# Output projection of a hybrid encoder layer: seven products of quarters in place of eight, with the residual added on GpSimd

## The chip, the cores and the metric

The kernel runs on one core of a Trainium2 chip. The core has a matrix engine (TensorE, PE in the profile, with its weight loads as PEld), a vector engine (VectorE, DVE), an activation engine (ScalarE, ACT), GpSimd (POOL) and SyncE (SP), which here only issues DMAs. Each engine works through its own queue in order; semaphores join them. The metric is the device time of one execution in microseconds, and the median of several executions is compared.

## The reference

One layer: a pre-norm, one input projection, two mixers that run side by side (chunked band attention and a gated delta rule), an output projection with a residual, and a feed-forward block with a residual. The part at issue is the output projection:

```python
mixed = jnp.concatenate([o_att, o_dn], axis=-1) @ w_out[layer]
h = h + mixed
z = rms_norm(h, ffn_norm_gain[layer]) @ w_ff1[layer]
h = h + jnp.square(jax.nn.relu(z)) @ w_ff2[layer]
```

Tokens, model width and the width of the two mixers together are all 1024, so the projection is a product of two 1024 x 1024 matrices in float32.

## The kernel before, in words

Everything is kept transposed: features on the 128 partitions, tokens along the rows. A float32 product is made of three matmuls: `split` (L201) writes a rounded copy of an operand with a cast on ACT (the high part) and the rest with a subtract on DVE (the low part), and `mm3` (L217) multiplies high by high, low by high and high by low.

The mixers leave four quarters in SBUF, each 512 features by 512 tokens: `mix[0][0]` and `mix[1][0]` from the attention (names `mixa0`, `mixa1`), `mix[0][1]` and `mix[1][1]` from the delta rule (`mixd0`, `mixd1`); the first index is the half of the tokens. `out_weights` (L1193) loads a half of W_out's columns, eight blocks of 128 x 512, through three buffers (tag `wr`). `out_proj` (L1199) makes four quarters of h, `R[j, hf]` (half j of the features, half hf of the tokens), each of four row tiles of 128 x 512: a row tile takes eight blocks of 128 times three matmuls in one PSUM bank; DVE adds the residual x to it on the way out (L1229), ACT squares it, POOL sums the squares (L1236), a DMA stores the quarter (L1237), and ACT scales it by the gain of the next norm (L1239) for the feed-forward block. The order is (0,0), (1,0), (1,1), (0,1), 384 matmuls in all.

The projection begins while the last units of the attention and of the delta rule still run. `attention` takes the generator's first steps (at most 30) as filling for PE between the units' own steps; the last unit is `t17`, the second group of four heads at token tile 7. Its normalization goes from PE (`t17_o`, then the transposes `t17_on`) through DVE, ACT (a square with its sum) and POOL (an inverse square root in small steps `t17_v`, `t17_y`, `t17_t`, `t17_r`) back to DVE, to PE (the transposes `t7_tpo`), and to DVE (L1070), which writes the last tile of `mixa1`. The order of instructions on each engine is set when the program is built, by a scheduler that simulates it; `issue_after` and priorities in the code shape it. PSUM for the projection is a pool of three banks, taken in turn.

The feed-forward block already uses seven products in place of eight for its matrices (`product` in `ff1` and `ff2`); it begins with `R[0, 0]`, goes on with `R[1, 0]`, and its first DVE work on sums of quarters is at L1290.

Of the kernel before, what the change touches and what calls it, by code (L numbers as in the profile page):

```python
# [14 lines left out]
P = 128  # L15
# [21 lines left out]
SPREAD = 5  # L37
WARM = 11
# [60 lines left out]
def hymba_kernel(  # L99
# [106 lines left out]
    lo_turn = [0]  # L206

    def load_w(src, name, tags=("wh", "wl"), low=None):
        raw = page("wr", name + "_r")
        nc.sync.dma_start(out=raw, in_=src)  # L210
        hi = page(tags[0], name + "_h", F32R)
        lo = page(tags[1], name + "_l", F32R)
        lo_turn[0] += 1
        split(raw, hi, lo, nc.scalar, low or (nc.gpsimd if lo_turn[0] % 2 else nc.vector))
        return hi, lo
# [977 lines left out]
    def out_weights(w, j):  # L1193
        w.append([None] * NKT)
        for k in order:
            w[j][k] = load_w(w_out[k * P:(k + 1) * P, j * 512:(j + 1) * 512], f"wo{j}_{k}",
                             (("wh", "u"), ("u", "wl"))[j], nc.vector)

    def out_proj(result, w):  # L1199


        parts, R, begun = [], {}, []

        def mixed(hf):
            parts.append([None] * NKT)
            low = [quarter(f"ml1{b}", F32R) for b in range(2)] if hf else None
            for j, k in enumerate(order):
                src = part(mix[hf][k // 4], k % 4)
                hi = page("u" if hf else ("pp", "cv")[k // 4], f"mh{hf}{k}", F32R)
                lo = part(low[k // 4], k % 4) if hf else page("dk", f"ml{hf}{k}", F32R)  # L1210
                with ExitStack() as queue:
                    if not hf:
                        for copies in turned:
                            queue.enter_context(tc.issue_after(copies[j // 2 - SPREAD]))
                    split(src, hi, lo, nc.scalar, nc.vector)
                parts[hf][k] = hi, lo

        def rows(j, hf, acc):
            R[j, hf] = r = quarter(f"h{j}{hf}")
            for i in range(4):  # L1220
                n = f"op{j}{hf}{i}"
                s = slice(i * P, (i + 1) * P)
                xt = page("wr", n + "_x")
                nc.sync.dma_start(out=xt, in_=x_t[4 * j + i, :, hf * TH:(hf + 1) * TH])
                ps = bank(ps_a, n)
                for m, k in enumerate(order):
                    mm3(ps, [((w[j][k][0][:, s], w[j][k][1][:, s]), parts[hf][k])], m == 0, m == NKT - 1)
                    yield
                nc.vector.tensor_tensor(part(r, i), ps, xt, ALU.add)  # L1229
                if i == 0 and acc is None:  # L1230
                    acc = page("on", n + "_q")
                    begun.append(nc.scalar.activation(acc, part(r, i), AF.Square).ins)
                else:
                    sq = page("wh", n + "_q")
                    nc.scalar.activation(sq, part(r, i), AF.Square)  # L1235
                    nc.gpsimd.tensor_tensor(acc, acc, sq, ALU.add)  # L1236
            nc.sync.dma_start(out=h_dr[j, hf], in_=q4(r))  # L1237
            for i in range(4):
                nc.scalar.mul(part(r, i), part(r, i), fgain[:, 4 * j + i:4 * j + i + 1])  # L1239
            return acc  # L1240

        mixed(0)
        acc = yield from rows(0, 0, None)
        out_weights(w, 1)
        acc = yield from rows(1, 0, acc)
        nc.sync.dma_start(out=sq_dr[:, 0:TH], in_=acc)
        mixed(1)
        acc = yield from rows(1, 1, None)
        acc = yield from rows(0, 1, acc)
        nc.sync.dma_start(out=sq_dr[:, TH:SEQ], in_=acc)  # L1250
# [425 lines left out]
```

## Time and profile before

| | |
|---|---|
| median of 3 runs | 1267.04 us (1262.9 to 1267.42) |
| the profiled execution | 1262.15 us, of which its span 1260.4 us |
| granted TensorE clock | 0.998 |
| chain that ended last | PE 55%, DVE 5%, ACT 1%; `op L222` (the projection) 7% |
| output projection, first to last matmul | 542.1 to 636.9 us |
| its matmuls | 3 x 128 of 128x512 |

In the profile an L number is a line of the kernel, `out<-in` are the names of the tiles without their numbers, and `xN` counts instructions. The chain of work that ended last is followed back from the last instruction to what released it at each step; where it stays on PE for long, PE had no pause. The output projection's matmuls are the rows `op L222`, its casts and subtracts the rows L203 and L204 with `wo`, `mh` and `ml`.

### The profile page before, as it was taken

To read this page: it belongs to the slowest core of one execution; us is meant where nothing else is said; L and a number is where in the kernel's file an instruction comes from. 1 tells how busy PE (TensorE), PEld (TensorE's weight loads), DVE (VectorE), ACT (ScalarE), POOL (GpSimd) and SP (SyncE) were. 2 spreads that over 40 slices of the span, in tenths; PEclk is the share of its full clock that TensorE was granted. 3 is DMA by queue.
4 is the path that set the end of the run, shared out by engine and by line. 5 is a ranking of instruction groups with operands and counts; after the bars stand their busy time and mean duration, and the time that the engine had idled before them with its cause. 6 is when DMAs were issued, how large, how long until landed. Compare 5 with 4: busy or idle time off the path is not lost.

```text
span 1260.4 us, 17948 instructions
## 1 busy us (share of the span) xinstructions
PE 1237.4 (98%) x6686; PEld 1030.8 (82%) x6686; DVE 929.2 (74%) x1397; ACT 547.4 (43%) x899; POOL 278.3 (22%) x478
## 2 busy tenths in 40 slices
PE   9999999999999999899999999999999999999997
PEld 8778878788789898788888788888887888888886
DVE  7899987754227568776269766767769997997998
ACT  8233132242236666665355444454445543333330
POOL 4425461343223445533200000000000000000043
PEclk9999999999999999999999999999999999999999
DMA  7214353664676532145242343333259624332002
GB/s 228 65 42 137 101 155 93 142 155 117 192 232 167 169 105 76 35 126 170 89 142 99 103 133 118 117 133 102 71 202 377 197 70 134 102 99 101 1 34 100
DMA packets 134375, 158.53 MB, mean 126 GB/s; under 512 B 31120, under 2 KB 78224, under 8 KB 133776
## 3 DMA queue, kind: packets, MB, share of 16 engines
q1 hardware_dynamic: 116192, 135.11, 35.3%
q10 hardware_dynamic: 18096, 22.29, 5.2%
q8 instruction: 52, 0.85, 0.3%
q14 instruction: 35, 0.29, 0.1%
HBM read 109.91 MB, written 47.45 MB: 125 GB/s over the span
## 4 chain that ended last, share of the span: by engine, by line
PE 55%; DVE 5%; ACT 1%; issue 1%; POOL 0%; DVEq 0%
PE p L1444 23%; PE q L1348 20%; PE op L222 7%; PE t_o L1026 1%; DVE h L1290 1%; PE t_sa L927 0%; DVE q_0a_l L204 0%; PE t_tpb L987 0%; PE t_tpa L1003 0%; PE t_sb L927 0%; ACT t_pb L966 0%; PE c_pv L516 0%; PE c_po L516 0%; PE t_tpo L520 0%; PE c_pq L516 0%
## 5 line engine op out<-in xcount | busy, mean ns | idle before, releaser
L1516 POOL TENSOR_TENSOR y<-y,y 128x1024 f32<-128x1024 f32 x4 | 11.5, 2896 | 575.6 <-DVE y L1512 570.8
L1512 DVE TENSOR_TENSOR y<-y,p 128x1024 f32<-128x1024 f32 x46 | 55.1, 1214 | 5.1 <-PE p L1444 4.1
L222 PE MATMUL op<-ml,wo_h 128*128 128x512 f32 x128 | 50.2, 395 | 0.0
L222 PE MATMUL op<-mh,wo_h 128*128 128x512 f32 x128 | 49.2, 393 | 0.8 <-ACT mh L203 0.8
L222 PE MATMUL op<-mh,wo_l 128*128 128x512 f32 x128 | 49.2, 391 | 0.0
L947 DVE CUSTOM_DVE_ANT_0 t_pb<-t_sb,biasn 128x256 f32<-128x256 f32 (+1 forms) x64 | 23.2, 400 | 30.1 <-DMA vt<-v_dr 27.0
L966 ACT ACTIVATE t_pb<-t_pb,t_nm 128x256 f32<-128x256 f32 (+1 forms) x64 | 31.4, 491 | 17.5 <-DVE t_nm L958 16.0
L1236 POOL TENSOR_TENSOR op_q<-op_q 128x512 f32<-128x512 f32 x14 | 20.7, 1478 | 54.6 <-ACT op_q L1235 54.3
L1229 DVE TENSOR_TENSOR h<-op,op_x 128x512 f32<-128x512 f32 x16 | 10.8, 687 | 29.2 <-PE op L222 29.1
L222 PEld LDWEIGHTS op<-mh,wo_h 128*128 128x128 f32 x128 | 23.9, 188 | 6.4 <-ACT mh L203 1.0
L222 PEld LDWEIGHTS op<-ml,wo_h 128*128 128x128 f32 x128 | 24.0, 188 | 5.1 <-DVE ml L204 0.2
L222 PEld LDWEIGHTS op<-mh,wo_l 128*128 128x128 f32 x128 | 24.1, 188 | 5.0
L222 PE MATMUL g_ps<-uh,wg_h 128*128 128x512 f32 x64 | 25.3, 396 | 1.5 <-ACT wg_h L203 1.5
L958 DVE CUSTOM_DVE_ANT_0 t_pa<-t_sa,biaso,t_nm 128x384 f32<-128x384 f32 (+2 forms) x48 | 24.9, 543 | 2.3 <-PE t_sa L927 2.0
L970 ACT ACTIVATE t_pa<-t_pa,t_nm 128x384 f32<-128x384 f32 (+2 forms) x48 | 26.4, 550 | 0.0
L927 PE MATMUL t_sb<-ks,t_q 128*128 128x256 f32 (+1 forms) x144 | 23.9, 294 | 1.9 <-DVE t_nm L947 1.3
L222 PE MATMUL g_ps<-uh,wg_l 128*128 128x512 f32 x64 | 25.2, 393 | 0.4 <-POOL wg_l L204 0.4
L222 PE MATMUL aq_ps<-waq_h,uh 128*128 128x512 f32 x64 | 25.5, 399 | 0.0
L222 PE MATMUL dq_ps<-uh,wdq_h 128*128 128x512 f32 x64 | 25.5, 398 | 0.0
L222 PE MATMUL dv_ps<-uh,wdv_l 128*128 128x512 f32 x64 | 25.4, 397 | 0.0
L222 PE MATMUL aq_ps<-waq_l,uh 128*128 128x512 f32 x64 | 25.3, 395 | 0.0
L222 PE MATMUL dq_ps<-ul,wdq_h 128*128 128x512 f32 x64 | 25.3, 395 | 0.0
(1110 smaller groups left out, 4302.7 us busy)
## 6 DMA issues: line engine op xcount, KB each, us to landing
wa<-in_w_ff_dram SPq DMA_DIRECT2D x32, 512.0 KB, 3.9
a<-in_w_ff_dram SPq DMA_DIRECT2D x32, 512.0 KB, 3.8
b<-f_dr SPq DMA_DIRECT2D x32, 512.0 KB, 3.4
f_dr<-yy ACTq DMA_DIRECT2D x16, 512.0 KB
t_q<-q_dr SPq DMA_DIRECT2D x30, 256.0 KB, 4.1
f_dr<-zz ACTq DMA_DIRECT2D x13, 512.0 KB
ks<-k_dr SPq DMA_DIRECT2D x16, 256.0 KB, 5.3
wo_r<-in_w_out_dram SPq DMA_DIRECT2D x16, 256.0 KB, 5.2
```

The costliest lines, as they stand in the source:

```text
L222: nc.tensor.matmul(ps, a, b, start=(first and i == 0), stop=(last and i == n - 1))
L927: nc.tensor.matmul(o, q[m][:, i * P:(i + 1) * P], k[:, c], start=(m == 0), stop=(m == 1))
L947: nc.vector.tensor_tensor_reduce(sb[:, c], bk[:, c], new[g][pp][:, c], -1.0, 3.0e38, ALU.add, ALU.min, nm[:, 4 + i:5 + i])
L958: nc.vector.tensor_tensor_reduce(sa[e][:, 0:wa], bk[:, 0:wa], old[g][i][:, 384 - wa:384], -1.0, nm[:, 4 + i:5 + i], ALU.add, ALU.min, nm[: ...
L966: nc.scalar.activation(sb[:, c], sb[:, c], AF.Exp, bias=m, scale=-1.0, accum_out=T["sums"][:, 4 + i:5 + i])
L970: nc.scalar.activation(sa[e][:, 0:wa], sa[e][:, 0:wa], AF.Exp, bias=m, scale=-1.0, accum_out=T["sums"][:, i:i + 1])
L1026: return nc.tensor.matmul(po[64 * e:64 * e + 64, pp * P:(pp + 1) * P], vt[k0 + j][:, 64 * h:64 * h + 64], (ta[e] if j < na else tb)[:, c:c ...
L1236: nc.gpsimd.tensor_tensor(acc, acc, sq, ALU.add)
L1290: nc.vector.tensor_tensor(t, wide(R[a], i), wide(R[b], i), ALU.subtract)
L1348: nc.tensor.matmul(part(ps, q), l[:, s], r, start=(k + m == 0), stop=(k == 3 and m == 2))
L1444: nc.tensor.matmul(part(ps[q], 0) if by_rows else part(ps[q // 2], q % 2), l[:, s], part(r, k), start=(i + k + m == 0), stop=(i + k + m == 4))
L1512: nc.vector.tensor_tensor(y[i][m], y[i][m], ps[m], op)
```

## The change

The product of the two matrices, each cut into quarters, is computed by Winograd's form of Strassen's scheme: seven products of quarters (p1, p2, p5, p6, p7, p4, p3 in the order of the program) with sums and differences of quarters in front of and behind them. A product has four row tiles of four blocks times three matmuls, 48 in all. W_out's quarters a11, a12, a21, a22 are loaded anew for the sums (`s1` = a21 + a22, `s2` = s1 - a11, `s3` = a11 - a21, `s4` = a12 - s2); those of the mixers are combined in place (`t1` to `t4`). s1 and s2 are made on POOL, the other differences on DVE; all eight blocks of operands of a product are split on ACT and DVE. DVE or ACT empty the banks into `oy1` and `oy5` (partial results) and into the quarters of h; POOL adds the residual x to them, block by block, and joins `oy5` and `oy1`. The loads for the sums go through the two-buffer pages that the delta rule (`jq`, `jv`, `jg`) and the attention (`raw`) used. The loads of the feed-forward weights are issued behind the first load of x.

The diff, cut to its core:

```diff
+        def product(n, a, b, use):
             for i in range(4):
                 s = slice(i * P, (i + 1) * P)
+                ps = bank(ps_a, f"{n}_{i}")
+                for m in range(4):
+                    mm3(ps, [((a[m][0][:, s], a[m][1][:, s]), b[m])], m == 0, m == 3)
                     yield
+                use(i, ps)
...
+        def residual(t, j, hf, i, tag="wr"):
+            xt = page(tag, f"x{j}{hf}{i}", w=516 if tag == "raw" else 512)[:, 0:512]
+            ins = nc.sync.dma_start(out=xt, in_=x_t[4 * j + i, :, hf * TH:(hf + 1) * TH]).ins
...
+            nc.gpsimd.tensor_tensor(t, t, xt, ALU.add)
...
+        def done(j, hf, last):
+            nc.sync.dma_start(out=h_dr[j, hf], in_=q4(R[j, hf]))
             for i in range(4):
+                nc.scalar.mul(part(R[j, hf], i), part(R[j, hf], i), fgain[:, 4 * j + i:4 * j + i + 1])
...
+        def use2(i, ps):
...
+            tt(part(R[0, 0], i), part(y1, i), ps, ALU.add)
+            residual(part(R[0, 0], i), 0, 0, i)
+            squared(0, 0, i)
...
+        def use6(i, ps):
+            tt(part(y1, i), part(y1, i), ps, ALU.add)
+            nc.gpsimd.tensor_tensor(y5[i], y5[i], part(y1, i), ALU.add)
+            residual(part(y1, i), 1, 0, i)
+
+        def use7(i, ps):
...
+            tt(part(R[1, 1], i), y5[i], ps, ALU.add)
+            tt(part(y1, i), part(y1, i), ps, ALU.add)
+            residual(part(R[1, 1], i), 1, 1, i, J[i])
+            residual(y5[i], 0, 1, i, J[i])
+            squared(1, 1, i)
...
+        yield from product("p1", w[4:8], lo[0:4], use1)
+        yield from product("p2", w[0:4], lo[4:8], use2)
+        done(0, 0, False)
...
+        for m in range(4):
+            with tc.issue_after(w_loads[-1]):
+                r1, r2 = raw(J[m], "a21", 1, 0, m), raw(J[m], "a22", 1, 1, m)
+            S.append(page("pp" if m < 3 else "cv", f"os{m}"))
+            nc.gpsimd.tensor_tensor(S[m], r1, r2, ALU.add)
+            a.append(halves(S[m], f"s1{m}", "u", "wl"))
+            tt(part(b11, m), part(b12, m), part(b11, m), ALU.subtract)
+            b.append(halves(part(b11, m), f"t1{m}", "u", "u"))
+        yield from product("p5", a, b, use5)
...
+            nc.gpsimd.tensor_tensor(S[m], S[m], r1, ALU.subtract)
+            a.append(halves(S[m], f"s2{m}", "wl", "u"))
+            tt(part(b11, m), part(b22, m), part(b11, m), ALU.subtract)
+            b.append(halves(part(b11, m), f"t2{m}", "pp", "dk"))
+        yield from product("p6", a, b, use6)
...
+        yield from product("p7", a, b, use7)
+        done(1, 1, False)
...
+        yield from product("p4", a, b, use4)
+        done(1, 0, True)
...
+        yield from product("p3", a, b, use3)
+        done(0, 1, True)
```

How the built order moves, at the three places that count. The first is the end of the attention on PE. Before, around the transposes `t17_on`, with `op003` and `op100` row tiles of the projection:

```order
L222 MATMUL op003_6760<-mh03_6622,wo0_3_h_6416 128x512
L222 MATMUL op003_6760<-ml03_6623,wo0_3_h_6416 128x512
L1051 MATMUL t17_on_6652<-ident_138,t17_pb1_6347 128x128 x2
L222 MATMUL op003_6760<-mh03_6622,wo0_3_l_6417 128x512
L222 MATMUL op100_6845<-mh04_6594,wo1_4_h_6796 128x512
L222 MATMUL op100_6845<-ml04_6595,wo1_4_h_6796 128x512
```

and around `t7_tpo`, 42 projection matmuls later:

```order
L222 MATMUL op102_6907<-mh05_6598,wo1_5_h_6802 128x512
L222 MATMUL op102_6907<-ml05_6599,wo1_5_h_6802 128x512
L520 MATMUL t7_tpo_6717<-ident_138,t04_on_4606 128x128 x4
L222 MATMUL op102_6907<-mh05_6598,wo1_5_l_6803 128x512
L222 MATMUL op102_6907<-mh06_6602,wo1_6_h_6808 128x512
```

And now, with `p2_2` and `p2_3` the third and fourth row tile of product p2:

```order
L223 MATMUL p2_2_6762<-ml3_6624,wo0_3_h_6416 128x512
L223 MATMUL p2_2_6762<-mh3_6623,wo0_3_l_6417 128x512
L1052 MATMUL t17_on_6650<-ident_138,t17_pb1_6347 128x128 x2
L521 MATMUL t7_tpo_6715<-ident_138,t04_on_4606 128x128 x4
L223 MATMUL p2_3_6782<-mh0_6611,wo0_0_h_6398 128x512
```

The matmuls between the two transposes are gone; p2_3 takes the bank of p2_0 and waits for DVE's `h00<-oy1,p2_0`. On DVE and POOL the last unit's steps now stand among the operands of the next products. DVE now, from the scale of `t04_on` (the tile that `t7_tpo` transposes) on, with `c11_r` and `c21_r` freshly loaded blocks of W_out:

```order
L1328 TENSOR_TENSOR c11_r1_7063<-c11_r1_7063,c21_r1_7065 128x512
L1061 TENSOR_SCALAR t04_on_4606<-t04_on_4606,t17_r_6661 128x512
L205 TENSOR_TENSOR s30_l_7054<-c11_r0_7048,s30_h_7053 128x512
L1328 TENSOR_TENSOR c11_r2_7078<-c11_r2_7078,c21_r2_7080 128x512
L1328 TENSOR_TENSOR c11_r3_7093<-c11_r3_7093,c21_r3_7095 128x512
L1071 TENSOR_TENSOR mixa1_6201<-t7_tpo_6715,again_286 128x4x128
L1267 TENSOR_TENSOR h00_6735<-oy1_6594,p2_0_6722 128x512
```

POOL now, where before a single 128x512 sum of squares stood between `t17_v` and `t17_r`:

```order
L1309 TENSOR_TENSOR os3_6856<-a21_r3_6852,a22_r3_6854 128x512
L188 TENSOR_SCALAR t17_v_6656<-t17_oss_6654 128x1
L1318 TENSOR_TENSOR os0_6811<-os0_6811,b11_r0_6927 128x512
L1318 TENSOR_TENSOR os1_6826<-os1_6826,b11_r1_6939 128x512
L190 TENSOR_TENSOR t17_y_6658<-t17_v_6656,mhalf_151 128x1
L1318 TENSOR_TENSOR os2_6841<-os2_6841,b11_r2_6951 128x512
L1318 TENSOR_TENSOR os3_6856<-os3_6856,b11_r3_6963 128x512
L193 TENSOR_TENSOR t17_t_6660<-t17_y_6658 128x1
```

Five blocks of POOL work stand in front of or among the small steps. The second place is ACT ahead of product p6, whose operands are the splits of `s2` and `t2`; `sq003` is the square of the last tile of `R[0, 0]`, `t30_h` to `t33_h` and `s32_h` are high parts for p7, `oy5_2` a result of p5:

```order
L1249 ACTIVATE sq003_6799<-h00_6735 128x512
L204 CAST t30_h_7058<-mixd1_5953 128x512
L204 CAST t31_h_7073<-mixd1_5953 128x512
L204 CAST t32_h_7088<-mixd1_5953 128x512
L204 CAST t33_h_7103<-mixd1_5953 128x512
L1273 COPY oy5_2_6910<-p5_2_6897 128x512
L204 CAST s32_h_7083<-c11_r2_7078 128x512
```

DVE splits the same blocks in this order, and its four low parts of `t2` (`t20_l` to `t23_l`) stand behind them; p6's third matmul reads `t20_l`. The third place is ACT ahead of product p3. Before, the scaling of a stored quarter stood among squares of later tiles:

```order
L1235 ACTIVATE op113_q_7120<-h11_6999 128x512
L1239 ACTIVATE h11_6999<-h11_6999,fgain_278 128x512 x4
L1235 ACTIVATE op010_q_7157<-h01_7128 128x512
L1235 ACTIVATE op011_q_7188<-h01_7128 128x512
L1235 ACTIVATE op012_q_7219<-h01_7128 128x512
```

Now the high parts of p3's operands (`s40_h`, `b220_h`) are behind it:

```order
L1249 ACTIVATE sq102_7296<-oy1_6594 128x512
L1255 ACTIVATE h11_7120<-h11_7120,fgain_278 128x512 x4
L204 CAST q2_0a_h_7585<-wa12_0_7508 128x1024
L1249 ACTIVATE sq103_7313<-oy1_6594 128x512
L204 CAST s40_h_7325<-e12_r0_7322 128x512
L204 CAST b220_h_7329<-mixa1_6201 128x512
```

The scaling waits for the store of `h11`, and the store for POOL's residual add to `h11`'s last tile; p3's first matmul reads `b220_h` and `s40_h`.

140 lines of the change are left out of this document (88 added, 52 removed).

## The prediction

> **What bounds the kernel now.** The page's first part comes first, then the stage of the output projection by itself, since the change is worth what that stage makes of it: the busy times of its window and PE's waits in it.
>
> ```profile
> PE 1237.4 (98%) x6686; PEld 1030.8 (82%) x6686; DVE 929.2 (74%) x1397; ACT 547.4 (43%) x899; POOL 278.3 (22%) x478
> ...
> 541.00:637.00 96.00, 95.19 (x463) 77.96 (x462) 46.17 (x67) 42.48 (x74) 27.40 (x33) 1.00 0.39 126
> ...
> PE op L222 <- ACT mh L203: 0.8, 1, 0.8
> ```
>
> PE is busy 95.19 of the 96 us of the stage and waits there once, 0.8 us. DVE has 46.17 us of work in it, ACT 42.48, POOL 27.40: half or less. So a matmul that is left out is worth its full pitch here, as long as the other engines keep delivering. The chain that ended last shows that pitch, and the end of the stage:
>
> ```profile
> 562.53 2.34 PE t_o L1026 x40
> 564.87 5.44 PE op L222 x23
> ...
> 570.53 9.56 PE op L222 x42
> 580.09 0.44 PE t_tpo L520 x4
> 580.53 56.46 PE op L222 x247
> 636.98 5.24 PE q L1348 x23
> ...
> 645.47 0.49 DVE h L1290
> ...
> 570.15 0.38 PE L1051 MATMUL t_on<-ident,t_pb 128*128 128x128 f32 x2
> ```
>
> 56.46 / 247 = 0.229 us for a 512-column matmul. From `t_o`, the last attention product, to the first feed-forward matmul PE runs without a pause. Note the third row: between the transposes `t_on` (570.15, the last row, from the timeline) and `t_tpo` (580.09) of the last attention tile PE had 42 projection matmuls. They cover that tile's normalization.
>
> **What is removed.** Seven products of 48 matmuls stand for eight: 48 x 0.229 = **11.0 us** less for PE. 79 matmuls stand ahead of `t_o` where 72 did, so `t_o` ends (T0 below) about 1.5 us later and 257 matmuls are left behind it.
>
> **What is added.** Loads of W_out rise from 16 to 36, the splits and differences are on ACT and DVE, and POOL gets 28 adds of 128x512 beside its 14 sums of squares. Their prices:
>
> ```profile
> L1236 POOL TENSOR_TENSOR op_q<-op_q x14: 1281/1294/2356, 563.2 to 638.6; 128x512 f32<-128x512 f32 x14
> ...
> L203 ACT CAST wo_h<-wo_r x16: 604/620/622, 522.2 to 581.1; 128x512 fp32r<-128x512 f32 x16
> ...
> 585.96 3.59 DVE L204 TENSOR_TENSOR ml<-mixd,mh 128x512 fp32r<-128x512 f32 x4
> ...
> 586.85 1.55 POOL L1236 TENSOR_TENSOR op_q<-op_q 128x512 f32<-128x512 f32 x1 [8.87 <-ACT op_q L1235]
> ...
> 589.47 2.48 DVE L204 TENSOR_TENSOR ml<-mixa,mh 128x512 fp32r<-128x512 f32 x4
> ```
>
> A POOL add is 1.29 us alone, a DVE subtract 2.48 / 4 = 0.62, a cast 0.62 (0.55 in a row of several). The same four subtracts take 3.59 with one POOL add among them: 1.11 more, nearly the whole add. **POOL and DVE take turns on operands in SBUF.** POOL now has some 40 such operations in about 80 us, DVE some 64 (39.7 us).
>
> Three waits of PE follow from the order of the rows.
>
> **W1, in front of product p2's last row tile.** PE now has `t7_tpo` straight behind `t17_on`: the 42 matmuls that covered it are gone, and p2_3 needs the bank that DVE empties only behind `mixa1`. The durations of that normalization:
>
> ```profile
> 574.47 0.19 POOL L187 TENSOR_SCALAR t_v<-t_oss 128x1 f32<-128x1 f32 x1 [8.63 <-ACT t_on L1058]
> 574.74 0.56 POOL L189 TENSOR_TENSOR t_y<-t_v,mhalf 128x1 f32<-128x1 f32 x1
> ...
> 576.51 0.64 POOL L192 TENSOR_TENSOR t_t<-t_y 128x1 f32<-128x1 f32 x1
> ...
> 577.79 0.19 POOL L199 TENSOR_TENSOR t_r<-t_y,t_t 128x1 f32<-128x1 f32 x1
> ...
> 578.01 0.49 DVE L1060 TENSOR_SCALAR t_on<-t_on,t_r 128x512 f32<-128x512 f32 x1 [0.91 <-POOL t_r L199]
> ...
> 582.47 0.69 DVE L1070 TENSOR_TENSOR mixa<-t_tpo,again 128x512 f32<-128x512 f32 x1
> ...
> 566.49 0.33 SPq L210 DMA_DIRECT2D wo_r<-in_w_out_dram  x1
> ...
> 569.08 0.62 ACT L203 CAST wo_h<-wo_r 128x512 fp32r<-128x512 f32 x1 [1.43 <-DMA wo_r<-in_w_out_dram]
> ...
> wo_r<-in_w_out_dram SPq DMA_DIRECT2D x13, 256.0 KB, 5.2
> ```
>
> Counted from T0: the load `a22_r3` goes into a buffer that `t_o` reads to its end, and lands 2.6 later (569.08 - 566.49) at 2.7. Everything on PE stands behind p2_3, so nothing runs in the meantime. POOL's row then is os3 (to 4.0), `t17_v` (4.2, its square long done), two adds (6.8), `t17_y` (7.4), two adds (10.0), four small steps (1.5, as from 576.51 to 577.98) to 11.5. DVE's follows: scale 0.49, three subtracts 1.9, `mixa1` and the first `h00` 0.69 each: 15.2. Eight splits and differences of DVE fall between POOL's adds, up to 5.0 us if all of them hold POOL up; DVE often waits there for its own inputs, so I take half: 17.7. PE has 5 matmuls, `t_on` and `t_tpo` to do meanwhile, 1.9. **W1 = 15.8**; 13.3 with nothing shared, 20.9 with all of it and a load of 5.2.
>
> **W2, in front of p6.** Counted from the start of p2_3, p5 ends at 60 x 0.229 = 13.7, and two matmuls of p6 run to 14.2. The third needs `t20_l`. DVE has it behind the splits of p7's operands; those wait for ACT's `t30_h`; in front of that ACT has `sq003`, which waits for the fourth residual add. POOL's seven adds (9.0) and DVE's twelve subtracts (7.4) are 16.4 one after the other; then come `sq003` and `t30_h` (1.2), five ACT operations to `s32_h` (2.75), five DVE splits (3.05): 23.4, a wait of 9.2. Were nothing shared, the add would follow DVE's 9.4 at once: 17.7 and a wait of 3.5. I take **W2 = 8**, near the shared end, since both queues are full there as in the row of 3.59.
>
> **W3, in front of p3.** ACT's rows put the scaling of `h11` ahead of `s40_h`, and the scaling waits for `h11`'s store. The rows for it:
>
> ```profile
> h_dr<-h SPq DMA_DIRECT2D x4, 1024.0 KB, 5.5
> ...
> 578.15 2.56 ACT L1239 ACTIVATE h<-h,fgain 128x512 f32<-128x512 f32 x4 [2.70 <-DMA h_dr<-h]
> ...
> 615.04 1.05 ACT L203 CAST q_0a_h<-wa 128x1024 fp32r<-128x1024 f32 x1 [4.08 <-PE op L222]
> ```
>
> Counted from the end of p6: PE is free after 96 x 0.229 = 21.9. POOL starts when DVE has emptied p6_0 (18 matmuls before the end, 0.69 to empty it), at -3.4; `h11`'s last residual is its 16th operation: 20.6 later, 17.2, and up to 6.8 more for eleven DVE operations between them; half is 20.6. Store 5.5, scaling 2.56, one cast of 1024 columns 1.05 and three operations of 0.62: 31.6. **W3 = 9.7** (6.3 to 13.1). Before, PE had enough work at this place.
>
> PE's restart after such a wait is not in this trace; its nearest rows are the launch:
>
> ```profile
> 1.05 5.07 PE L165 MATMUL warm<-ones 128*128 128x128 f32 x22 [1.05 <-POOL ones L160]
> ...
> 5.77 0.77 PE L362 MATMUL dk_ps<-uh,wdk_h 128*128 128x512 f32 x1
> 6.34 0.63 PE L362 MATMUL dk_ps<-ul,wdk_h 128*128 128x512 f32 x1
> 6.77 0.52 PE L362 MATMUL dk_ps<-uh,wdk_h 128*128 128x512 f32 x1
> 7.13 0.40 PE L362 MATMUL dk_ps<-ul,wdk_h 128*128 128x512 f32 x1
> ...
> PE p L1444 <- DVE p50b_l L204: 1.8, 1, 1.8
> ...
> 960.25 293.64 PE p L1444 x1294
> ```
>
> The first 22 matmuls take 0.21 us each where `t_tpo`'s take 0.11, and the next three 0.57, 0.43, 0.36 instead of 0.229: about 3 us lost from a standing start. Behind the 1.8 us wait there is no loss to see (293.64 / 1294 = 0.227). So a restart costs 0 to 3; I take 1.3 each behind W2 and W3 (behind W1 it only eats into W2), 2.5 in all. The Trainium skill, "TensorE: Matmul & The Clock Gate", part 1, says that an idle window of some 3.4 us halves the clock, and that as long a busy one restores it. By that each restart would lose 1.7 (an estimate from that page) and the forecast would be 0.9 higher; no wait of this trace is long enough to show it, though the launch agrees.
>
> The first feed-forward products have their operands in time: `b11` is split before p3 ends, and DVE's full stretch starts 8.5 us behind the stage's end, as before (row 645.47 of the chain against 636.98), give or take 1.
>
> **Sum.** -11.0 + 15.8 + 8 + 9.7 + 2.5 = **+25.0**. With nothing shared and no restart: -11.0 + 13.3 + 3.5 + 6.3 = +12.1. With everything: -11.0 + 20.9 + 9.2 + 13.1 + 6 = +38.2. The profiled execution took 1262.15, which gives 1287. The median of the runs shown, 1267.04, is 4.9 above it; for a median of new runs I add half of that: **1289**.
>
> **Rivals.**
> - A: POOL and DVE hardly disturb each other in these places. The other row for it is 1281, POOL's shortest, at a quiet DVE. +12.1: 1274 to 1280. Chance 0.20.
> - B: not slower. Its mechanism is POOL's queue at W3 and W2: if POOL works off its adds while PE stands in W1, only W1 is left, and at a floor of 11 (operands early, no DVE row in between) it equals the saving: 1262 to 1267. It decides itself at W3 where `h11`'s last add is done by 10.9 after p6 (21.9 - 5.5 - 2.56 - 2.9): 16 adds in 14.3 us, 0.9 each, below the shortest row of 1281. The busy tenths speak for it, the rows against it. Chance 0.12, a third of it faster.
> - C: full turns everywhere, loads of 5.2 and slow restarts: +38.2, 1296 to 1306. Chance 0.16. The Trainium skill, "SBUF — State Buffer", section on the two separate sides, calls the port pair of VectorE and GpSimd an exclusive lock: the loser blocks for a whole instruction. By that rule alone the shared ends of the three waits hold (18.3, 9.2, 13.1), an estimate of +32 with my restarts; the rows of 3.59 and 1.55 bear the rule out, but not that both queues are full throughout.
>
> **How the numbers follow.** My forecast holds 0.52 (1280 to 1296), A 0.20, C 0.16, B 0.12. The range 1274 to 1306 leaves out B and the tails of C. Half a per cent, 6.3 us, is about what a measurement of this kernel can tell from no change. Faster by more has a third of B, 0.04; within it 0.08; slower by more 0.88.
>
> **What would show it.** In the changed profile: PE waits of over 10 us at `t_tpo` and at p2 on DVE or POOL; one of some 8 at p6 on a DVE split of `t2`, one of some 9 at p3 on ACT, with ACT waiting for a store of `h`; POOL's 128x512 adds at 1.5 us or more in the mean; the first `q` matmul some 25 us later. If PE's waits between `t_o` and `q` sum to under 17 us, the forecast is wrong; if they come from loads that land late, the reason is.

## The result, and the profile after

The changed kernel takes **1297.2 us** in the median (1295.88 to 1299.5, four runs) where the kernel before takes 1267.23 beside it: a ratio of **1.0251** (95 % interval 1.0236 to 1.0266). It is slower by 2.5 %. The forecast was 1289, with a range of 1274 to 1306. The profiled execution took 1295.88 us, its span 1294.2; before it was 1262.15 and 1260.4. One execution further down, the profiled one of e_p3f, ran at a granted clock of 0.65 and took 1773 us; it is left out, and so is its trace.

The page's first row and its row of the granted clock:

```profile
PE 1240.4 (96%) x6638; PEld 1029.7 (80%) x6638; DVE 981.3 (76%) x1453; ACT 564.5 (44%) x931; POOL 318.2 (25%) x506
PEclk9999999999999999987989999999999999999999
```

PE has 48 instructions fewer, and yet 3.0 us more of busy time. The clock's row dips in slices 18, 19 and 21 (32.4 us each, so 550 to 615 and 647 to 679), the stage of the output projection. Its rows in the table of windows (length; then the busy times of PE, PEld, DVE, ACT and POOL; then the clock, the DMA share and GB/s): first the whole stage, from the first projection matmul to the first feed-forward one, then four stretches in it.

```profile
542.08:668.00 125.92, 95.85 (x411) 74.80 (x412) 93.45 (x119) 57.18 (x101) 66.45 (x60) 0.86 0.42 137
584.70:591.00 6.30, 6.23 (x15) 4.88 (x16) 6.30 (x7) 3.68 (x6) 6.15 (x4) 0.51 0.57 168
606.50:611.50 5.00, 4.92 (x12) 3.92 (x13) 1.83 (x4) 0.75 (x2) 0.00 (x0) 0.51 0.15 52
635.00:639.00 4.00, 4.00 (x11) 3.12 (x12) 3.80 (x5) 3.70 (x7) 3.58 (x4) 0.57 0.44 155
653.90:660.00 6.10, 5.59 (x14) 3.99 (x15) 5.36 (x8) 5.35 (x10) 0.95 (x1) 0.57 0.28 90
```

The same stage of the kernel before, cut in the same way:

```profile
542.11:636.82 94.71, 94.71 (x459) 77.72 (x460) 45.06 (x65) 41.37 (x71) 27.40 (x33) 1.00 0.38 123
```

The stage is 125.92 - 94.71 = **31.2 us longer**, out of the span's 33.8, and these rows split it. At the old pitch PE would need 94.71 - 11.0 = 83.7 us. It is idle for 125.92 - 95.85 = **30.1**. And its busy time is 95.85 - 83.7 = **12.1** longer than the work needs: the same matmuls, run slower. The four short rows show where: full of matmuls, at a clock of 0.51 to 0.57. At 0.229 us a matmul they hold 6.23 - 15 x 0.229 = 2.8, 2.2, 1.5 and 2.4 us of it, and the 0.65 us that `t_tpo` takes longer than before make 9.5; the other 2.6 are not put down to a place here. DVE's busy time in the stage has doubled, 45 to 93 us. Of the span's 33.8 us, the last 2.6 come later, at the start of the second feed-forward product: PE waits 2.9 us there instead of 1.8, and its 1294 matmuls behind that wait take 295.2 us instead of 293.6.

PE's waits in the stage from the end of the attention on, by group (what waited, for whom: us in all, times, the longest). Ahead of them there is one of 0.7 us, for a bank of p1.

```profile
PE t_tpo L521 <- DVE t_on L1061: 13.1, 1, 13.1
PE p L223 <- DVE t_l L205: 6.1, 4, 3.2
PE p L223 <- ACT b_h L204: 4.9, 1, 4.9
PE p L223 <- DVE h L1267: 1.8, 1, 1.8
PE p L223 <- DVE oy L1291: 1.2, 1, 1.2
PE p L223 <- ACT oy L1273: 1.2, 1, 1.2
PE p L223 <- DVE b_l L205: 0.5, 1, 0.5
PE p L223 <- DVE oy L1284: 0.5, 1, 0.5
```

By place they are: 13.1 + 1.8 = 14.9 at the end of the attention (W1), 1.2 + 3.2 = 4.4 at p6 (W2), some 4.7 at p4 (the other three of `t_l`, and `oy` L1284 and L1291), 4.9 + 0.5 = 5.4 at p3 (W3). What follows such a wait, from PE's timeline (start, duration, instruction, and in brackets the idle time before it and what ended it):

```profile
566.53 0.61 PE L1027 MATMUL t_o<-t_tb,vt 128*64 128x128 f32 x8
...
581.87 1.09 PE L521 MATMUL t_tpo<-ident,t_on 128*128 128x128 f32 x4 [13.14 <-DVE t_on L1061]
584.77 0.80 PE L223 MATMUL p<-mh,wo_h 128*128 128x512 f32 x1 [1.82 <-DVE h L1267]
...
585.79 0.63 PE L223 MATMUL p<-mh,wo_l 128*128 128x512 f32 x1
...
591.15 0.39 PE L223 MATMUL p<-t_h,s_h 128*128 128x512 f32 x1
...
606.58 0.80 PE L223 MATMUL p<-t_l,s_h 128*128 128x512 f32 x1 [3.15 <-DVE t_l L205]
```

Behind a wait the matmuls start 0.43 us apart instead of 0.23, for some 3 to 6 us, and then all at once at the full rate again (the step at 591).

Why W1 is as long as it is stands in POOL's timeline, beside the DVE instruction that it releases:

```profile
571.93 2.93 POOL L1318 TENSOR_TENSOR os<-os,b_r 128x512 f32<-128x512 f32 x2
574.82 1.00 POOL L190 TENSOR_TENSOR t_y<-t_v,mhalf 128x1 f32<-128x1 f32 x1
575.79 3.00 POOL L1318 TENSOR_TENSOR os<-os,b_r 128x512 f32<-128x512 f32 x2
...
581.23 0.49 DVE L1061 TENSOR_SCALAR t_on<-t_on,t_r 128x512 f32<-128x512 f32 x1
```

Two pairs of 128x512 differences stand between the small steps of the normalization for which PE waits. The sum `os3` in front of them started at 570.32, when its load had landed; POOL had stood 3.79 us for it.

### The profile page after: what moved, and what is told of

It reads as the page before. It is cut to its first block, busy times and chain, and to the rows that moved or that the text cites. A ratio compares the mean times of both kernels' runs of the same rounds, so it can differ in the third digit from the quotient of the medians.

```text
span 1294.2 us, 18012 instructions
## 1 busy us (share of the span) xinstructions
PE 1240.4 (96%) x6638; PEld 1029.7 (80%) x6638; DVE 981.3 (76%) x1453; ACT 564.5 (44%) x931; POOL 318.2 (25%) x506
## 4 chain that ended last, share of the span: by engine, by line
PE 44%; DVE 7%; issue 2%; DMA 1%; ACT 1%; POOL 0%; SPq 0%; DVEq 0%; POOLq 0%
PE p L1542 23%; PE q L1446 20%; PE p L223 2%; DMA a<-in_w_ff_dram 1%; DVE q_0a_l L205 1%; DVE t_l L205 0%; DMA d_r<-in_w_out_dram 0%; DVE mixd L1320 0%; DVE h L1387 0%; ACT h L1255 0%; DVE e_r L1343 0%; DVE mixd L1330 0%; DVE s_l L205 0%; DVE mixa L1325 0%; DVE h L1267 0%
## 5 line engine op out<-in xcount | busy, mean ns | idle before, releaser
L948 DVE CUSTOM_DVE_ANT_0 t_pb<-t_sb,biasn 128x256 f32<-128x256 f32 (+1 forms) x64 | 23.2, 400 | 30.1 <-DMA vt<-v_dr 27.0
L223 PE MATMUL dq_ps<-ul,wdq_h 128*128 128x512 f32 x64 | 25.3, 396 | 0.0
L223 PE MATMUL aq_ps<-waq_l,uh 128*128 128x512 f32 x64 | 25.3, 396 | 0.0
L223 PE MATMUL aq_ps<-waq_h,ul 128*128 128x512 f32 x64 | 25.3, 395 | 0.0
L223 PE MATMUL g_ps<-ul,wg_h 128*128 128x512 f32 x64 | 25.2, 396 | 0.0
L223 PE MATMUL dv_ps<-ul,wdv_h 128*128 128x512 f32 x64 | 25.2, 393 | 0.0
L223 PE MATMUL ak_ps<-wak_h,ul 128*128 128x512 f32 x64 | 25.1, 395 | 0.0
L223 PE MATMUL av_ps<-wav_l,uh 128*128 128x512 f32 x64 | 25.1, 395 | 0.0
L223 PE MATMUL dv_ps<-uh,wdv_h 128*128 128x512 f32 x64 | 25.1, 393 | 0.0
L223 PE MATMUL ak_ps<-wak_l,uh 128*128 128x512 f32 x64 | 25.1, 395 | 0.0
L223 PE MATMUL av_ps<-wav_h,uh 128*128 128x512 f32 x64 | 25.1, 395 | 0.0
```

Source lines behind the costliest of these rows:

```text
L223: nc.tensor.matmul(ps, a, b, start=(first and i == 0), stop=(last and i == n - 1))
L948: nc.vector.tensor_tensor_reduce(sb[:, c], bk[:, c], new[g][pp][:, c], -1.0, 3.0e38, ALU.add, ALU.min, nm[:, 4 + i:5 + i])
```

## The experiments

All ratios are to the kernel before, run on the same chip, with a 95 % interval. The third to fifth columns are of the profiled execution, from the first projection matmul to the first feed-forward one: its length, PE's idle time in it, and how much longer PE was busy than 83.7 us (for e_warm without the 5.4 us of its added matmuls). The last is DVE's busy time.

| kernel | ratio | stage, us | idle | dragged | DVE |
|---|---|---|---|---|---|
| before | 1 | 94.7 | 0.0 | - | 45.1 |
| after | 1.0251 (1.0236 to 1.0266) | 125.9 | 30.1 | 12.1 | 93.5 |
| e_os | 1.0209 (1.0190 to 1.0227) | 120.1 | 25.3 | 11.1 | 93.7 |
| e_res | 1.0141 (1.0126 to 1.0156) | 113.3 | 23.0 | 6.6 | 94.6 |
| e_scale | 1.0284 (1.0268 to 1.0299) | 124.9 | 28.2 | 13.0 | 94.0 |
| e_cover | 1.0207 (1.0190 to 1.0224) | 120.2 | 27.4 | 9.1 | 95.7 |
| e_p3f | 1.0237 (1.0220 to 1.0255) | | | | |
| e_warm | a single execution, 1291.15 us | 123.1 | 24.8 | 9.2 | 94.2 |
| b1_res_os_cover | 1.0131 (1.0114 to 1.0147) | 108.6 | 17.7 | 7.2 | 95.4 |
| b2_all | 1.0130 (1.0107 to 1.0153) | 102.1 | 12.4 | 6.0 | 91.4 |
| b3_early_on | 1.0078 (1.0056 to 1.0100) | 97.9 | 9.5 | 4.6 | 90.3 |
| b3_dma_residual | 1.0102 (1.0083 to 1.0121) | 101.6 | 11.6 | 6.4 | 79.9 |
| b4_rows | 1.0048 (1.0024 to 1.0072) | 100.7 | 12.1 | 4.9 | 96.0 |
| b5_banks_dma | 1.0021 (1.0011 to 1.0031) | 93.7 | 7.2 | 2.7 | 88.8 |

One caution for all of them: the first projection matmul starts at 542.08 us in the profiled execution of the changed kernel and between 542.8 and 547.7 in those of the experiments, although nothing ahead of it was edited. So each profiled execution carries an offset of up to 5.6 us that is no effect of the edit. Whether it belongs to the build or to the single execution is not shown; executions of the kernel before alone lie between 1262.7 and 1267.7 us in one series. The stage's length is free of the offset, the time of an execution is not.

### e_os: POOL's queue at W1

```diff
-            nc.gpsimd.tensor_tensor(S[m], r1, r2, ALU.add)
+            nc.vector.tensor_tensor(S[m], r1, r2, ALU.add)
...
-            nc.gpsimd.tensor_tensor(S[m], S[m], r1, ALU.subtract)
+            nc.vector.tensor_tensor(S[m], S[m], r1, ALU.subtract)
```

> The four sums and the four differences of W_out quarters (os) are done on VectorE instead of GpSimd; nothing else is edited. Theory (the order of the rows makes the waits): in the changed kernel GpSimd's row has os3 and four differences among the steps of t17's normalization, and t_on starts at 581.23. Without them t_on should start at 576 to 577, so the wait in front of t7_tpo falls from 13.1 to 8 or 9 us and the time by 4 to 6 us, to 1291 to 1293. Rival (only the missing cover counts, and VectorE takes up the same work): t_on stays within 1 us of where it is, time within 1 us of 1297.2. Rival (the gain is given back): t_on earlier by 4 us or more, but p6 starts no earlier than 606 us, and the time is the same.

The wait at `t_tpo` falls from 13.1 to 6.1 us, and the ratio by 0.0042, some 5 us. The wait for `h` behind it grows from 1.8 to 2.4, so the sums and differences in POOL's queue make 6.4 us of W1's 14.9. Some 1.8 us are given back further on: 0.7 in p5 and at p6, where PE now waits for copies of ACT, and 1.1 at p4.

```profile
PE t_tpo L521 <- DVE t_on L1061: 6.1, 1, 6.1
...
PE p L223 <- ACT oy L1273: 4.7, 2, 3.2
```

### e_res: the residual back on VectorE

```diff
-            nc.gpsimd.tensor_tensor(t, t, xt, ALU.add)
+            nc.vector.tensor_tensor(t, t, xt, ALU.add)
...
-            nc.gpsimd.tensor_tensor(y5[i], y5[i], part(y1, i), ALU.add)
+            nc.vector.tensor_tensor(y5[i], y5[i], part(y1, i), ALU.add)
```

> The sixteen residual adds and the four sums oy5 + oy1 are done on VectorE instead of GpSimd. Theory (GpSimd's row of adds holds up VectorE and the store that the scaling of h11 waits for): the VectorE split that took 5.59 us at 626.26 takes 0.7, the wait at p3 on the scaling (4.9 us) and its slow restart go, p4's waits (1.9 and 0.9) shrink: 5 to 9 us less, 1288 to 1292. Rival (VectorE is the bound of this stage): it gets 20 x 0.62 = 12.4 us more work, and the waits at p6, p4 and p3 grow by as much as they lose or more: 1297 to 1307.

This gains 0.0110, some **14 us** (12.6 of them in the stage), the largest single effect of the changes tried one by one, and more than was expected. From the end of the attention on PE has these four waits in the stage:

```profile
PE t_tpo L521 <- DVE t_on L1061: 13.3, 1, 13.3
PE p L223 <- ACT b_h L204: 6.7, 1, 6.7
PE p L223 <- DVE h L1267: 1.8, 1, 1.8
PE p L223 <- DVE t_l L205: 0.4, 1, 0.4
```

All waits at p4 are gone and the one at p6 nearly so; the one at p3, which the theory had go, is still there, and longer. By the table 7.1 us of the gain in the stage are waits and 5.5 are matmuls that no longer run slowly behind them. DVE's busy time hardly grows, from 93.5 to 94.6, though it has 20 operations more: the others have become shorter. The changed kernel's timeline ahead of p4 shows why:

```profile
626.24 2.59 POOL L1240 TENSOR_TENSOR oy<-oy,x 128x512 f32<-128x512 f32 x2
626.26 5.59 DVE L205 TENSOR_TENSOR a_l<-d_r,a_h 128x512 fp32r<-128x512 f32 x1
628.73 1.34 POOL L1240 TENSOR_TENSOR h<-h,x 128x512 f32<-128x512 f32 x1
629.98 1.33 POOL L1240 TENSOR_TENSOR oy<-oy,x 128x512 f32<-128x512 f32 x1
```

A subtract of DVE that starts beside POOL's adds ends only 5.59 us later, behind the fourth of them. That long turn is no rule: of the five kernels here that keep these adds on POOL and have a trace, only the changed kernel has it. In e_warm, where the order of POOL and DVE at this place is the same, the same subtract and the next one read:

```profile
625.89 1.86 DVE L205 TENSOR_TENSOR a_l<-d_r,a_h 128x512 fp32r<-128x512 f32 x1
627.67 1.78 DVE L205 TENSOR_TENSOR t_l<-mixa,t_h 128x512 fp32r<-128x512 f32 x1
```

There each subtract ends behind one add. But the four subtracts that stand here in a row take 6.9 us in e_warm and 7.4 in the changed kernel, and PE waits at p4 in both. Without adds beside it, in e_res, the first takes 0.69:

```profile
623.48 0.69 DVE L205 TENSOR_TENSOR a_l<-d_r,a_h 128x512 fp32r<-128x512 f32 x1
```

So the two engines take turns, mostly one by one and once four to one, and it is DVE's splits for p4 that stand in these turns. The Trainium skill, "SBUF — State Buffer", section on the two separate sides, has the shared port pair as an exclusive lock held for a whole instruction. The turns agree: a subtract of 0.69 us takes 1.78 to 1.86 beside an add of 1.29 us.

### e_scale: the scaling of h11 behind p3's casts

```diff
+            if (j, hf) != (1, 1):
+                scaled(j, hf)
...
+        with tc.issue_after(last_cast[0]):
+            scaled(1, 1)
         yield from product("p3", a, b, use3)
```

> The scaling of h11 on ScalarE stands behind the casts of p3's operands instead of ahead of them; nothing else moves before p3. Theory: p3's first products waited 4.9 us for the cast b_h behind that scaling (648.84 to 651.39), and restarted slowly (about 2 us); both go but for 0 to 1 us: 5 to 7 us less, 1290 to 1292. Rival (the casts' own inputs, or VectorE's splits of them, are as late): p3 starts within 1 us of 656, time within 1.5 us of 1297.2.

The expected gain does not come. The stage is only 1.0 us shorter, and the ratio is worse by 0.0033, some 4 us. Its profiled execution reaches the stage 5.6 us later than the changed kernel's (the first projection matmul starts at 547.68), ahead of the edit; the others have no trace. Its waits at p3:

```profile
PE p L223 <- ACT b_h L204: 2.5, 1, 2.5
...
PE p L223 <- DVE b_l L205: 1.3, 1, 1.3
```

They are 3.8 us in place of 5.4. ACT's timeline of the changed kernel shows what held the casts:

```profile
645.97 1.23 ACT L1249 ACTIVATE sq<-oy 128x512 f32<-128x512 f32 x2 [4.50 <-DVE oy L1291]
...
648.84 2.55 ACT L1255 ACTIVATE h<-h,fgain 128x512 f32<-128x512 f32 x4
...
653.27 0.61 ACT L204 CAST b_h<-mixa 128x512 fp32r<-128x512 f32 x1
```

The scaling has no wait of its own, so the store that it needs was not what held the casts. Its own 2.55 us did stand ahead of them: without them the wait for `b_h` is 2.4 us shorter. The rest comes from the squares of p4's results in front of the casts. ACT is idle 4.50 us ahead of the first of them, until DVE has emptied p4's first banks (L1291). Of the 2.4 us, DVE's `b_l` takes back 0.8, and p4 ends 0.4 later.

### e_p3f: p3's operands ahead of those squares as well

```diff
-        yield from product("p4", a, b, use4)
-        done(1, 0, True)
...
+        yield from product("p4", a, b, use4)
+        with tc.issue_after(last[0]):
+            for i in range(4):
+                squared(1, 0, i)
+            scaled(1, 1)
+            done(1, 0, True)
+        yield from product("p3", a3, b3, use3)
```

> The casts of p3's operands on ScalarE stand ahead of the squares of p4's result as well as of the scaling of h11 (moving the scaling alone left them behind those squares, which wait until p4 is emptied). Theory (ScalarE's row makes the wait at p3): p3 starts within 1 us of p4's end instead of 7 us later, with at most 1.5 us of waiting for the last load e12_r3, and without the slow restart of 2 us: 5 to 7 us less than the changed kernel, a ratio to the kernel before of 1.0195 to 1.0212. Rival (VectorE, held up by GpSimd, brings the differences e12 or the splits as late): the ratio stays within 0.0015 of 1.0251.

1.0237 is 0.0014 below the changed kernel, within what the rival allowed: the expected gain is not seen. Without a trace, whether W3 went and came back elsewhere was not seen here; b2_all below has the same edit.

### e_cover: matmuls of p5 back in front of `t7_tpo`

```diff
+                if t == NT - 1:
+                    for _ in range(48 - fill):
+                        next(outputs_gen)
+                    queue.enter_context(tc.issue_after(last_mm[0]))
+                tp = bank(ps_t, f"t{t}_tpo")
+                four_t(tp, head(o))
...
-            tt(part(R[0, 0], i), part(y1, i), ps, ALU.add)
+            t = page("dk", f"oy2_{i}")
+            nc.scalar.copy(t, ps)
+            tt(part(R[0, 0], i), part(y1, i), t, ALU.add)
```

> p5's 48 matmuls, which need nothing of the last attention tile, are put ahead of its transpose t7_tpo; p2 is emptied by copies on ScalarE, because the quarter that h00 needs is held by t7_on until that transpose. Theory: the wait in front of t7_tpo (13.1 + 1.8 us, and 3.7 us of slow restart) falls to 2 or 3 us ahead of p5. But p6 still waits for t20_l, which stands some 17 us behind mixa1 in VectorE's and ScalarE's rows: p6 starts at 600 to 602 us instead of 606.6, and the time falls by 4 to 7 us only, to 1290 to 1293: the wait moves from t7_tpo to p6. Rival (the missing cover alone makes the loss): the wait goes and nothing takes its place: 14 to 18 us less, 1279 to 1283.

The wait at `t_tpo` is gone, 13.1 us, and the stage is 5.7 us shorter. The rest moves to p6, as the theory had it (7.6 us and the 8.0 of the first row; the two other waits of that row are at p4):

```profile
PE p L225 <- DVE t_l L205: 11.8, 3, 8.0
PE p L225 <- ACT t_h L204: 7.6, 1, 7.6
```

Work that covers one wait of PE brings PE sooner to the next, as long as DVE and ACT deliver no faster.

### e_warm: the price of the slow clock alone

```diff
         yield from product("p4", a, b, use4)
...
+        keep = bank(ps_t, "keep")
+        with tc.issue_after(last_mm[0]):
+            for i in range(24):
+                ins = nc.tensor.matmul(keep, old[0], old[1], start=True, stop=True).ins
```

> 24 matmuls of p4's operands into a bank that nobody reads stand between p4 and p3, 5.5 us, inside the wait of 7 us; all else up to p3 is as in the changed kernel. Theory (an idle TensorE restarts at about half its clock): p3's first matmuls, 0.43 us apart in the changed kernel, come at 0.229, and the last of p3 ends about 2 us sooner counted from the first. Rival (the first matmuls are slow because their operands trickle in): they stay at 0.43.

24 matmuls whose result nothing reads fill the wait ahead of p3. p3 in the chain of this kernel, and the window of its first 24 matmuls:

```profile
654.80 11.20 PE p L225 x48
```

```profile
654.70:660.00 5.30, 5.30 (x24) 4.18 (x23) 4.47 (x8) 4.38 (x8) 0.00 (x0) 1.00 0.28 99
```

p3 now runs at 11.20 / 48 = 0.233 us each with a clock of 1.00. In the changed kernel the chain has, behind its waits at p6 and p3:

```profile
606.58 8.88 PE p L223 x28
...
656.06 12.11 PE p L223 x45
668.17 5.24 PE q L1446 x23
...
676.65 1.06 DVE h L1387
```

8.88 - 28 x 0.229 = 2.5 us lost, and 12.11 - 45 x 0.229 = 1.8. So the loss behind a wait comes from PE having stood, not from its operands: with the same operands, and PE kept busy, it is gone. Product p2 shows the same: p2_2 had read every block that p2_3 reads, and p2_3's matmuls came 0.43 us apart behind W1. The Trainium skill, "TensorE: Matmul & The Clock Gate", part 1, says that the clock is halved after an idle window of some 3.4 us, and full again after a busy one as long; the stretches of 3 to 6 us at 0.51 to 0.57 agree. But one of them stands behind waits of 1.87, 0.24 and 0.46 us in a row at p4 (635 to 639), shorter than the page's window.

### b1_res_os_cover, b2_all, b3_early_on: the causes taken away together

b1 has e_res, e_os and a form of e_cover at once, with `t2` ahead of p7's operands on ACT and DVE and `R[0, 0]` behind them. b2 adds e_p3f's order. b3 puts what is left of p2 and p5 behind the transposes `t17_on` on PE:

```diff
+                if t == NT - 1:
+                    for _ in range(36 - fill):
+                        next(outputs_gen)
...
+        t2 = tuple(last)
+        with tc.issue_after(t2[0]), tc.issue_after(t2[1]):
+            first()
...
+                        if turned9 and n in ("p2", "p5"):
+                            queue.enter_context(tc.issue_after(turned9[0]))
```

> All adds on VectorE but the sums of squares; p5's first row tile ahead of t7_tpo and the other three behind it, as cover; the differences and splits of t2 first in VectorE's and ScalarE's rows behind mixa1, with h00, its squares and p7's operands behind them; p2 emptied by copies. Theory (order of rows): p6 starts 16 to 18 us behind t_o's end instead of 33.5 with the residual adds on VectorE alone; 10 to 17 us less than that kernel (ratio 1.0141): a ratio of 1.000 to 1.006. Rival (VectorE is full now, some 100 operations of 0.6 us in this stage): p7, p4 or p3 wait for its splits, and the ratio is 1.008 to 1.014.

> As b1, and the casts of p3's operands ahead of the squares of p4's result. Theory: 5 to 7 us less than b1, a ratio of 0.995 to 1.001. Rival (VectorE is full): the wait at p3 passes to its splits, the ratio is that of b1 within 0.0015.

> As b2, and the rest of p2 and all of p5 on TensorE stand behind the transposes t17_on of the last attention tile: in b2 these stood behind 17 matmuls and ran at 573.69, 4.4 us after their operand t_pb was ready at 569.34. Theory (the wait at t7_tpo is on the path): t_on 4 us earlier, the wait at t7_tpo of 6.2 us falls to 2 or 3, and the time by 3 to 5 us against b2 (ratio 1.0130), to a ratio of 1.009 to 1.0107. Rival (VectorE, busy without a gap from mixa1 to p3 in b2, is the bound): p7, p4 and p3 wait for its splits by as much more, and the ratio stays within 0.0015 of 1.0130.

The ratios are 1.0131, 1.0130 and 1.0078. b1 and b2 fall where the rival of each had put them, a VectorE that is full. b3 is below even what its theory had, and the same rival is out there: the kernel is faster with nearly the same work on DVE (90.3 us after 91.4). Idle time in the stage drops from 30.1 to 17.7, 12.4 and 9.5 us, step by step, and the drag behind the waits with it. But b2's gain in the stage (6.5 us over b1) is lost again behind it, where its kernel takes 6.8 us more. The larger part are new waits of PE for DVE and ACT in the first part of the feed-forward block, 1.9 + 1.5 + 0.7 us. So b2's rival had the time right and the place wrong: it had the wait pass to p3's splits, and at p3 only 1.2 us are left. With W3's casts early, other work of the same engines is late. b3's stage is 3.1 us longer than before's, and most of the rest of its 0.8 % lies behind the stage in the same way.

### b3_dma_residual: the residual by accumulating DMAs

```diff
-            xt = page(tag, f"x{j}{hf}{i}", w=516 if tag == "raw" else 512)[:, 0:512]
...
-            nc.vector.tensor_tensor(t, t, xt, ALU.add)
+            nc.gpsimd.dma_start(out=t, in_=x_t[4 * j + i, :, hf * TH:(hf + 1) * TH], accum_op=ALU.add)
```

> As b3_early_on, but the sixteen residual adds are done by DMAs that add in SBUF (issued on GpSimd's queue), so neither VectorE nor GpSimd computes them: VectorE has 16 x 0.6 = 9.6 us less work in the stage. Theory (VectorE is the bound of this stage): 5 to 9 us less than b3_early_on. If b3_early_on is at 1.009 to 1.013, this is at 1.002 to 1.008. Rival (another thing bounds it: order of rows, loads, ScalarE): within 0.0015 of b3_early_on. Third possibility: an adding DMA takes 5 us or more each and holds up the squares, the stores of h and the scalings: p7 or p3 waits longer and the ratio is above b3_early_on.

DVE's work falls by 10 us, and the kernel is not faster, 1.0102 against b3's 1.0078, as the third possibility had it. The page's rows of DMA issues (KB each, median us from issue to landing):

```profile
h<-in_x_t_dram POOLq DMA_DIRECT2D x8, 256.0 KB, 5.2
oy<-in_x_t_dram POOLq DMA_DIRECT2D x8, 256.0 KB, 5.1
```

5 us stand where DVE's add took 0.69. ACT's squares and the emptying of a bank of p7 wait for them (up to 7.9 and 2.4 us), and ACT's casts for p3, which stand behind the squares, are late again, 4.4 us.

### b4_rows, b5_banks_dma: the rest of the order

b4 is b3 with p7's operands split ahead of `R[0, 0]` and an early load for `s4`; b5 gives p6, p7, p4 and p3 six banks in turn instead of three, and the eight residual adds of `h00` and `h01` to DMAs.

```diff
-            r1 = raw("wr", "e12", 0, 1, m)
+            r1 = raw("cv", "e12", 0, 1, m)
...
-                ps = bank(ps_a, f"{n}_{i}")
+                late = n in ("p6", "p7", "p4", "p3")
+                ps = bank((ps_a, ps_a, ps_a, ps_d, ps_d, ps_o)[turns[0] % 6] if late else ps_a, f"{n}_{i}")
+                turns[0] += late
+            if (j, hf) in ((0, 0), (0, 1)):
...
+                nc.gpsimd.dma_start(out=t, in_=x_t[4 * j + i, :, hf * TH:(hf + 1) * TH], accum_op=ALU.add)
```

> As b3_early_on (ratio 1.0078), with three rows moved: the loads of e12 go to buffers that are free since p1 (in b3 the last one waited for a split of the one ahead of it and held ScalarE's row, 5.9 us idle in front of s43, and with it the squares, the scalings and the feed-forward part's first casts); p7's operands (t3, s3) are made ahead of h00 and its squares (in b3 p7 waited 1.6 us for the emptying of p6 and 1.5 and 0.7 for t3, with a slow restart of 1.5); mixa0's last difference stands behind h00. Theory (the order of the rows still costs time, on top of VectorE's load): 2 to 4 us at p7, 1 to 2 at p3, and up to 5 at the feed-forward part's head: a ratio of 0.999 to 1.004. Rival (VectorE is full from t7_tpo to the feed-forward part, whatever the order): p4, p3 or the head wait by as much more, and the ratio stays within 0.002 of 1.0078.

> As b4_rows (ratio 1.0048), with two things changed. The tiles of p6, p7, p4 and p3 take turns in six PSUM banks (three more, free since attention's end): in b4 p7 stood 6.03 us until p6's first bank was emptied, which VectorE did only behind eight operations of h00 and mixa0, and restarted slowly (2.2 us). And eight of the sixteen residual adds, those of h00 and of the fourth quarter's sum oy5, which nobody needs at once, are done by DMAs that add in SBUF: 8 x 0.6 = 4.8 us less for VectorE, which in b4 has no gap from 582 to 645 us. Theory (VectorE's load and its order are what is left): 4 to 9 us less than b4, a ratio of 0.998 to 1.002. Rival (the wait only passes to the next operand that VectorE makes, and GpSimd's descriptors and the landing of 5 us cost as much as they save): a ratio of 1.003 to 1.007.

b4's 1.0048 lies between its theory and its rival. Its stage is 2.9 us longer than b3's; the gain lies behind it, where b3's waits in the feed-forward block are gone. Its largest wait of PE is for a bank, which led to b5:

```profile
PE p L225 <- DVE oy L1302: 6.0, 1, 6.0
```

b5 is at **1.0021**, at the edge of what its theory had: the nearest of all, and still not below 1. Its stage, its waits, and the ACT instruction ahead of the longest:

```profile
543.82:637.49 93.67, 86.43 (x412) 70.27 (x413) 88.76 (x139) 54.91 (x99) 38.34 (x38) 0.96 0.60 182
```

```profile
PE p L225 <- ACT t_h L204: 5.4, 1, 5.4
PE q L1488 <- ACT q_1a_h L204: 2.2, 1, 2.2
```

```profile
609.49 2.56 ACT L1285 ACTIVATE h<-h,fgain 128x512 f32<-128x512 f32 x4 [4.15 <-DMA h_dr<-h]
```

The stage is now 1.0 us shorter than before's: 11.0 saved, 7.2 idle and 2.7 of slow clock against it. 1.7 us are the offset ahead of it, and the other 4.0 of its span's 4.7 us (1265.1 against 1260.4) come in the feed-forward block, where `q_1a_h` is late and PE runs slowly behind that wait. DVE is busy for 88.8 of 93.7 us. The wait of 5.4 us is the order of rows once more: ACT's casts for p4 behind a scaling that waits for a store. Whether an order without it would be faster than the kernel before was not tried.

## Why the prediction was right in direction and too low

**The saving, 11.0: right.** 48 instructions are gone, and at the full clock the pitch is the old one (0.233 in e_warm's p3).

**W1, 15.8: right, 14.9, its size in part by luck.** Its working also gave the place on the clock: the first matmul of p2_3 at 17.7 us behind the end of `t_o`. It starts at 584.77, and `t_o` ends at 566.53 + 0.61: 17.6. e_os shows POOL's share (6.4 us), e_cover that it was the lost cover. The 2.5 us for shared operands are met in sum and not in place: POOL's four differences lost only 0.7 us, its small steps 1.4 (2.4 us instead of 1.5 for the last four, 1.0 instead of 0.56 for `t_y`), and the load came 0.5 us later than forecast.

**W2, 8: right in place and cause, and its size is met once the clock is counted.** The forecast put p6's first matmul with `t20_l` 14.2 + 8 = 22.2 us behind the first of p2_3; it is 606.58 - 584.77 = 21.8. Only 4.4 of that is a wait, since p2_3 and the head of p5 ran slowly in between. That the restart behind W1 "only eats into W2" came true, and `sq003` does wait for POOL's residual add, as ACT's timeline below shows. But the two queues were not both full, as the forecast had taken it: POOL stood idle for 5.44 us ahead of that add, because DVE's twelve subtracts in front of its operand took 11.8 us instead of 7.4.

```profile
599.69 0.63 ACT L1249 ACTIVATE sq<-h 128x512 f32<-128x512 f32 x1 [2.97 <-POOL h L1240]
```

**The restarts, 2.5: the term that was mis-sized.** The stage's matmuls were dragged by 12.1 us. About 3.5 lie behind W1 and cost nothing (`t_tpo` 1.09 us instead of 0.44, 14 matmuls with 0.43 instead of 0.229). So some 6 to 8.6 are on the path (from 9.5 or 12.1), where I had two restarts of 1.3. I had the price low, taken between the launch and the unharmed 1.8 us wait of the feed-forward block: it was 2.5 behind W2 and 1.8 behind W3. At that place of the feed-forward block a wait of 2.9 now costs 1.6. And I had too few of them: p4 has one as well. e_warm shows that it is the standing of PE and not the operands.

**p4: missing from the forecast, 4.7 us of waits and a restart.** "POOL and DVE take turns" was right. The step that failed is that I followed the turns into POOL's queue alone, and into DVE's only at W2: at p4 I gave DVE's splits no wait at all. Ahead of p4 the four subtracts that should take 2.8 us take 7.4 beside POOL's adds. e_res takes the adds away, and all waits at p4 are gone. The means say the same. POOL's 28 adds took 1.42 us each, less than the 1.5 that the forecast gave as a sign; DVE's operations in the stage took 0.79 (93.45 / 119) against 0.68 in e_res (94.60 / 139).

**W3, 9.7: the wrong cause, and too large.** 5.4 us were measured. The step that failed is "the scaling waits for `h11`'s store": in the trace the scaling waits for nothing. Only its own 2.55 us were in the way, and e_scale, which moves it, gains 1.0 us in the stage. The other part are squares in front of the casts that wait for the emptying of p4. That is read from ACT's row and from b2, where no wait on `b_h` is left, but with other edits at the same time; e_p3f alone has no trace to show it.

**The head of the feed-forward block: right** (8.5 us from 668.17 to DVE's first `h` at L1387, 676.65). The 2.6 us at its second product were not foreseen.

**The sum.** Forecast from `t_o` on: -11.0 + 33.5 waits + 2.5 = +25.0. Measured in the stage: -11.0 + 30.1 idle + 12.1 dragged = +31.2, and 2.6 behind it. The waits came out near their sum by luck, with errors against each other (p4 added, W2 and W3 too large); the clock made the difference. Of the rivals, A and B are out: the adds don't leave DVE alone, and PE waits at W2 and W3 too. 1297.2 lies in C's band, 1296 to 1306, and just above the forecast's own, 1280 to 1296. C's slow restarts were right, its waits (20.9, 9.2, 13.1) too large.

**What the change is worth at its best.** Much of the idle time is the order of rows and the place of the adds: with it taken out step by step, 2.5 % of loss came down to 0.2 %. What stays is, as far as the rows tell, VectorE. The matmuls saved are 11.0 us of PE; the sums, differences, splits and partial results put DVE from 45 to some 90 us in a stage of 95, so what is late there has little room to be made up. That last step is argued and not shown: b3 gained 4 us in the stage with hardly less work on DVE, and b3_dma_residual, with 10 us less on DVE and 5 us more behind each add, doesn't settle it.

## What to carry to other kernels

A product saved on an engine that is full is worth its pitch only while the engines that feed it have room: add up their work in that stage first, and then go through the rows for whatever small step now stands behind a large one. Elementwise work moved to GpSimd did not relieve VectorE here, where both read SBUF at the same time: it cost 14 us against having the same adds on VectorE. Follow the turns into both queues, and see which of them the next product reads from. In this kernel PE's waits from some 2 us on cost another 1.5 to 2.8 us of slow clock behind them, unless the next wait hid that.

## What the hardware showed that was not expected

- A VectorE subtract of 0.69 us took 1.8 to 1.9 beside GpSimd's adds in four kernels, and 5.59 beside four adds in a row in a fifth.
- PE ran at about half its clock (0.57) at p4 behind waits of 1.87 us and less, and at 0.51 behind 3.15. It came back in one step, after 3 to 6 us.
- Accumulating DMAs of 256 KB took 5.1 to 5.2 us from issue to landing.
- Kernels that were not edited ahead of the stage reached it 0.7 to 5.6 us later than the changed kernel, each in a single profiled execution.
